# Second layer's sq and kv projections as seven quadrant products, with sums of the normalized input taken from PSUM

## The chip, the cores and the metric

The kernel runs on one core of a Trainium2 chip. The metric is the device time of one execution in microseconds (us); the lower, the better. TensorE (PE) multiplies matrices into PSUM, VectorE (DVE) and ScalarE (ACT) do elementwise work and read PSUM, GpSimd (POOL) does small arithmetic on SBUF and issues some DMAs, and SyncE (SP) issues all the others. Each engine works through its own list of instructions in order; semaphores make one wait for another.

## What is computed

Two layers of a decoder trunk with 512 tokens and width 1024, in float32. Each layer normalizes its input, projects it once to 3488 columns, hands these columns to four groups of heads, gates each group, and projects the result back onto the residual.

```python
def hybrid_layer(x, ...):
    h = rmsnorm(x, norm_g)
    p = h @ w_in                      # (512, 1024) @ (1024, 3488)
    (cq, ckv, kr, g_a, c_h, c_b, c_c, g_b, sg_u, sg_v, g_c, mq, mk, mv, g_d) = jnp.split(p, offs, axis=-1)
    ...                               # o_a latent attention, o_b convolution, o_c spatial gate, o_d block attention
    y = jnp.concatenate([o_a * silu(g_a), o_b * silu(g_b), o_c * silu(g_c), o_d * silu(g_d)], axis=-1)
    return y @ w_out                  # added to x
```

Every matrix operand is kept as a high and a low part (`split2`), and a product is three matmuls (`mm3`): high x high, high x low, low x high.

## The kernel before

**The order of the work.** The kernel is a list of chains (Python generators). While it is built, `Order` keeps a clock for each engine and lets the chain that is due go on, so the order of instructions on each engine is fixed before the run by this plan. `Chain.act`, `Chain.dve` and `Chain.pool` emit at line 162, `Chain.pe` at line 188; nearly every row of the profile has one of these lines, so rows are told apart by tile names. `Slots` hands out buffers.

**One layer.** `pre_norm` scales the tokens (tile `h`), transposes them on PE into PSUM (`hT`, from the two banks of `trS`) and splits them into `hTh` and `hTl`. `main` then issues the long projections. `cq` (416 columns) comes first, for each of the four tiles of 128 tokens; `low_chain`, `q_chain` and `kv_chain` follow behind it on the other engines, with short PE work of their own (`cT`, `q`, `kv` of a latent rank). After it `main` goes through `SEQ`: the token projections `sq` (columns of `sv` and `mq`) and `kv` (`mk` and `mv`), and 16 features of 128 columns each (`ga0`, `su0`, `ch0` and so on). A token projection is 4 tiles x 8 blocks of the inner dimension x 3 matmuls of 512 columns; a feature is 8 x 3 = 24 matmuls of 512 columns. Their sums stand in the three banks of `accS`.

**Beside it.** When all of cq's followers are done, `mla_heads` starts the latent attention (`t0a`, `t1a` transposes, `sa` scores, `pTa` transposed weights, `oa` output), and when mq, mk, mv and the latent heads are done, `moba_heads` starts the block attention (`tmqd`, `sd`, `pTd`, `od`). `mix_chain` prepares the spatial gate (`sgw`, `wsh`, `wsl`, `mp`). Their PE work is put between the projections' matmuls. `put_y` splits each gated output into `yTh`/`yTl` (tiles 0 to 5) or `yD` (6 and 7), and sends it to DRAM (`ysc`, line 858).

**The output product** (`seven`) is made of seven quadrant products already, in both layers: `b11`, `t3`, `b21`, `t4`, `t2`, `t1`, `b22`, in the banks `oz`, `ox`, `oy`. The sums of its weights (`t_sums`) are made in DRAM: SP copies a quadrant (line 324), POOL adds another with an accumulating DMA (line 330). The sums of its left side are made by `s_chain` from the y that it reads back from `ysc` (tiles `ys`, `sumh`, `suml`); they take the place of `hTh` and `hTl`, so they can't start before the last projection is issued.

**Weights.** `load_units` loads units of 512 KB in the order of use, on SP, into `raw` buffers (two of `rawS`, some in `tkS`). `split_units` makes `whi` and `wlo` of each, in halves, as soon as ACT and DVE have time by the plan or the unit is among the next four wanted; six pairs of buffers (`wS`) hold them. Three units of sq (`EARLY`) go to `yTh`/`yTl`, which are empty then.

Of the kernel before, what the change touches and what calls it, by code (L numbers as in the profile page):

```python
# [42 lines left out]
ZPROD = ("b11", "t3", "b21", "t4", "t2", "t1", "b22")  # L43
TS0 = 36000.0
TAIL = ((0, 256), (256, 512))

# [154 lines left out]
def hybrid_trunk(ctx: ExitStack, tc: tile.TileContext, x, positions, norm_g, w_c, w_f, w_t, w_o, mla_q_norm_g,  # L201
# [115 lines left out]

    def t_sums(l):

        for steps in ((("t1", "b11", "b12"), ("t3", "b12", "b22")), (("t2", "t1", "b22"),), (("t4", "t2", "b21"),)):  # L320
# [12 lines left out]
            yield o.now + 8000.0  # L333
# [6 lines left out]
    for l in range(DEPTH):  # L340
# [3 lines left out]
        add_unit(mla_w_ukv[l], 1, 512, f"ukv_{l}")  # L344
        for n in SEQ:
            if n in TOKS:
# [13 lines left out]
    def load_units():  # L360
        for u in order:
            ch = Chain(o)
            u.raw_slots = rawS
            if u.name in ("c2_0", "c3_0") or u.name[:-3] in ZPROD and u.name[-3] == "1":
# [191 lines left out]
    for l in range(DEPTH):  # L556
# [16 lines left out]
        L.seven = l in SEVEN  # L573
        L.hT_free, L.p1, L.h_done, L.h = Event(), Event(), [Event(), Event()], {}
        L.s = {n: [Event() for _ in range(4)] for n in ("t2", "t1", "b22")}
        L.left, L.s4 = {}, [Event(), Event()]
        L.QK_taken = False
        L.torder = (2, 3, 0, 1) if l and layers[l - 1].seven else (0, 1, 2, 3)
        L.x = [None] * NT
        for n in ("ga0", "ga1", "gd0", "gd1"):  # L580
            L.gate_ev[n] = Event()
        for j in range(2):
            L.u_ev[j] = Event()
            L.b_ev[j] = [Event() for _ in range(3)]
        layers.append(L)

# [8 lines left out]
    def pre_norm(L, t, xx, t0, release):  # L595
# [18 lines left out]
        def half(c):  # L614
# [12 lines left out]
            o.set(L.hT[t][c], c2.t)  # L627
        for c in range(2):
            o.spawn(half(c))

    def hk(L, k):
# [144 lines left out]
    def sv_chain(L, t, a, t0, put):  # L776
        ch = Chain(o, t0)
        l = L.l
        if t == 0:
            L.vn = [(yield from v4S.get(ch, f"vnh{l}", [P, NT, GW], F32R)),  # L780
# [19 lines left out]
    def mix_chain(L):  # L800
        ch = Chain(o)
        l = L.l
        sgw = yield from obS.get(ch, f"sgw{l}")
        sgw = sgw.rearrange("p (g s) -> p g s", g=4)
# [11 lines left out]
        for g2 in range(2):  # L816
            mp = yield from accS.get(ch, f"mp{g2}_{l}")
            for g in (2 * g2, 2 * g2 + 1):
# [7 lines left out]
            accS.put(c2)  # L826
        t2S.put(ch)
# [16 lines left out]
    def put_y(ch, L, kt, yv):  # L844
# [135 lines left out]
    def mqk_chain(nm):  # L980
        def f(L, t, a, t0, put):
            ch = Chain(o, t0)
            l = L.l
            gn = L.dq if nm == "mq" else L.dk
            if t == 0:
                L.MD[nm] = yield from ydS.get(ch, f"{nm}{l}", [P, NT, 4, 64], F32)
# [22 lines left out]
    def mv_chain(L, t, a, t0, put):  # L1009
        ch = Chain(o, t0)  # L1010
        if t % 2 == 0:
            L.Mt[t // 2] = yield from v4S.get(ch, f"Mt{t}_{L.l}", [P, 2, 4, P], F32R)
# [307 lines left out]
    def main():  # L1320
# [17 lines left out]
        def done_unit(name):  # L1338
            if units[name].slots is not eS:
                units[name].slots.put(m)  # L1340

        def seven(L):
            l = L.l
# [68 lines left out]
        for L in layers:  # L1412
# [19 lines left out]
            for n in SEQ:  # L1432
                if n in TOKS:
                    us = []
# [27 lines left out]
            for half in range(0 if L.seven else 2):  # L1462
# [17 lines left out]
                for group, cut in (((0, 1, 2), YCUT), ((3,), 0)) if half == 0 else (((t,), 0) for t in range(NT)):  # L1480
# [83 lines left out]
    if 0 in SEVEN:  # L1564
        o.spawn(t_sums(0), TS0, 4)
    o.spawn(start())
    o.run()
# [50 lines left out]
```

## Time and profile before

| | us |
|---|---|
| median of 3 runs (lowest, highest) | 498.12 (497.85, 498.44) |
| the profiled execution | 499.12 |
| its span, first to last instruction | 497.4 |
| second layer: cq starts on PE | 255.61 |
| sq starts | 282.66 |
| kv starts | 319.81 |
| first of su0 | 358.19 |
| last matmul of attention | 429.75 |
| output product starts | 455.71 |
| its fifth product (t2) starts | 477.47 |

The starts are from the chain of waits and the timeline of PE. The page gives each engine's busy time; the chain of waits goes back from the last instruction to what released each; windows give the busy time of each engine in a stretch, with the clock that PE was granted and the busy share of the 16 DMA engines. A row of the timeline has the start, the length, the engine, the line, the operation, the tile written and those read, the shape, how many in a row, and in brackets the idle time before it with what ended it. A row's length on PE is that of one matmul in the pipeline; the step from one start to the next is what counts for the sum.

### The profile page before, as it was taken

The page shows a single profiled execution, that of the slowest core. Times are in us where ns is not written, and L with a number is a line of the kernel's source. Part 1 is how long each engine was busy: PE and PEld are TensorE (multiplying, and loading weights), DVE is VectorE, ACT ScalarE, POOL GpSimd, SP SyncE. Part 2 cuts the span into 40 slices and gives each one's busy share as a digit, 9 for nine tenths or more (in the row PEclk, how much of TensorE's full clock was granted, in tenths as well). Part 3 has the DMA queues.
Part 4 walks back from the last instruction along what each step waited for, and adds up shares of the span by engine and source line. Part 5 has one row for each costly group of instructions (what it writes and reads, how often), then busy time and mean ns, then how long its engine had stood idle before and what let it go on. Part 6 is the DMA issues. An engine that isn't in the chain of part 4 may idle for free.

```text
span 497.4 us, 7832 instructions
## 1 busy us (share of the span) xinstructions
PE 486.4 (98%) x2448; PEld 412.5 (83%) x2448; DVE 386.0 (78%) x1008; ACT 317.0 (64%) x933; POOL 156.2 (31%) x328
## 2 busy tenths in 40 slices
PE   6899999999999999999999999999999999999997
PEld 4798878788888888888889988888888888888886
DVE  4877884777988788669898698677969788765992
ACT  5688753576777775446657896567758587524640
POOL 6867883656110000000031388463351000000000
PEclk9999999999999999999999999999999999999999
DMA  8545559444575235786474232664548528565642
GB/s 273 150 141 199 196 117 203 171 86 88 192 145 188 71 98 175 210 299 219 157 256 157 86 106 108 211 149 97 118 122 245 142 102 215 174 249 188 227 171 92
DMA packets 35339, 81.98 MB, mean 165 GB/s; under 512 B 7137, under 2 KB 16609, under 8 KB 35042
## 3 DMA queue, kind: packets, MB, share of 16 engines
q1 hardware_dynamic: 26818, 73.10, 42.7%
q0 software_dynamic: 8480, 8.39, 11.5%
q8 instruction: 19, 0.31, 0.3%
q14 instruction: 22, 0.18, 0.1%
HBM read 73.61 MB, written 24.64 MB: 198 GB/s over the span
## 4 chain that ended last, share of the span: by engine, by line
PE 87%; POOL 4%; ACT 3%; DMA 3%; DVE 2%; issue 1%; POOLq 0%; DVEq 0%
PE kv L188 7%; PE cq L188 6%; PE oy L188 6%; PE sq L188 5%; PE cb L188 4%; PE gd L188 4%; PE ch L188 4%; PE cc L188 4%; PE su L188 4%; PE gc L188 4%; PE gb L188 4%; PE ox L188 4%; PE oz L188 4%; PE sa L188 3%; PE ga L188 2%; PE od L188 2%
## 5 line engine op out<-in xcount | busy, mean ns | idle before, releaser
L162 ACT ACTIVATE pd<-pd,mnd 128x256 f32<-128x256 f32 (+3 forms) x50 | 26.9, 547 | 2.8 <-DVE mnd L162 2.3
L330 POOL DMA_DIRECT2D t<-in_w_o_dram x16 | 17.9, 1121 | 33.1 <-DMA t<-t 22.6
L162 ACT ACTIVATE pha<-pTa 128x512 fp32r<-128x512 f32 (+3 forms) x32 | 13.9, 436 | 20.0 <-PE pTa L188 19.8
L188 PE MATMUL kv<-whi_kv,hTh 128*128 128x512 f32 x64 | 26.1, 408 | 0.0
L188 PE MATMUL kv<-whi_kv,hTl 128*128 128x512 f32 x64 | 25.1, 392 | 0.0
L188 PE MATMUL kv<-wlo_kv,hTh 128*128 128x512 f32 x64 | 25.0, 391 | 0.0
L188 PE MATMUL cq<-whi_c,hTh 128*128 128x416 f32 x64 | 24.0, 376 | 0.0
L162 ACT ACTIVATE phd<-pTd 128x512 fp32r<-128x512 f32 (+3 forms) x32 | 13.8, 434 | 14.9 <-PE pTd L188 14.7
L162 ACT ACTIVATE pa<-pa,mna 128x256 f32<-128x256 f32 (+3 forms) x40 | 21.4, 542 | 2.5 <-DVE mna L162 2.4
L188 PE MATMUL cq<-whi_c,hTl 128*128 128x416 f32 x64 | 22.6, 353 | 0.0
L188 PE MATMUL cq<-wlo_c,hTh 128*128 128x416 f32 x64 | 22.5, 351 | 0.0
L162 DVE TENSOR_TENSOR wlo_t<-raw_t,whi_t 128x512 fp32r<-128x512 f32 x32 | 21.1, 691 | 0.0
L162 ACT ACTIVATE whi_t<-raw_t 128x512 fp32r<-128x512 f32 x32 | 18.2, 618 | 4.1 <-DMA raw_t<-t 4.1
L162 POOL TENSOR_SCALAR xss<-xss 128x1 f32<-128x1 f32 x8 | 3.8, 476 | 52.3 <-ACT jk L162 45.1
L162 DVE TENSOR_TENSOR pla<-pTa,pha 128x512 fp32r<-128x512 f32 (+3 forms) x32 | 15.2, 484 | 5.5 <-ACT pha L162 5.5
L188 PE MATMUL sq<-yTh,hTh 128*128 128x512 f32 x48 | 18.9, 393 | 0.0
L188 PE MATMUL sq<-yTh,hTl 128*128 128x512 f32 x48 | 18.7, 390 | 0.0
L162 DVE TENSOR_TENSOR pld<-pTd,phd 128x512 fp32r<-128x512 f32 (+3 forms) x32 | 15.2, 484 | 4.5 <-ACT phd L162 4.4
L188 PE MATMUL sq<-yTl,hTh 128*128 128x512 f32 x48 | 18.7, 390 | 0.0
L162 DVE CUSTOM_DVE_ANT_0 pa<-sa,maskb 128x512 f32<-128x512 f32 (+3 forms) x32 | 14.8, 484 | 5.0 <-PE pTa L188 4.2
L162 DVE TENSOR_TENSOR wlo_b<-raw_b,whi_b 128x512 fp32r<-128x512 f32 x24 | 16.0, 688 | 0.7 <-ACT whi_b L162 0.7
L162 DVE CUSTOM_DVE_ANT_0 pd<-sd,maskb 128x256 f32<-128x256 f32 (+3 forms) x32 | 15.0, 483 | 2.0 <-PE pTd L188 1.9
(377 smaller groups left out, 1853.0 us busy)
## 6 DMA issues: line engine op xcount, KB each, us to landing
t<-in_w_o_dram POOLq DMA_DIRECT2D x16, 512.0 KB, 6.2
raw_t<-t SPq DMA_DIRECT2D x16, 512.0 KB, 4.0
raw_b<-in_w_o_dram SPq DMA_DIRECT2D x12, 512.0 KB, 4.2
raw_sq<-in_w_t_dram SPq DMA_DIRECT2D x8, 512.0 KB, 3.5
t<-in_w_o_dram SPq DMA_DIRECT2D x8, 512.0 KB, 4.4
raw_kv<-in_w_t_dram SPq DMA_DIRECT2D x8, 512.0 KB, 3.6
t<-t SPq DMA_DIRECT2D x8, 512.0 KB, 4.8
ys<-ysc SPq DMA_DIRECT2D x14, 256.0 KB, 5.2
```

Source lines behind the costliest of these rows:

```text
L162: f(*a, **k)
L188: f(*a, **k)
L330: nc.gpsimd.dma_start(z_src(l, n, j), quad(l, b, j), accum_op=ALU.add, max_dma_last_dim=1024)
```

## The change

The first layer stays. In the second (`STOK = (1,)`) sq and kv together are one product of a 512 x 1024 left side h and a 1024 x 1024 right side W, cut into quadrants: h11 (tokens 0 to 255, inner 0 to 511), h12, h21 and h22, and of W b11, b21 (columns of sq) and b12, b22 (of kv). Seven products replace eight: p11 = h11 b11; p21 = h12 b21; p3 = (h11 - h21)(b12 + b22); p4 = h22 (b11 + b12 + b21 + b22); p2 = (h11 - h21 + h22)(b11 + b12 + b22), p1 = (h21 - h22)(b11 + b12), p22 = (h12 - h11 + h21 - h22) b22. Each is 2 tiles x 4 blocks x 3 matmuls of 512 columns.

Four features stand between the products: ga0, ga1, gd0 and ch0; the 12 others follow p22. The sums of W are made in DRAM by `t_sums`, under the first layer (from 110 us by the plan). The sums of h are made by DVE from the transposes in PSUM before their bank is given back (`h_sums`), and split later (`sum_split`) into `yTh`/`yTl`; so the early units of sq and a y of tiles 0 to 5 wait for that space. `p_out` combines products: for each of two tiles of 128 tokens it copies p11, p3 and p4 on ACT and takes two differences for p2 and one for p1 on DVE. The second half of each pair of weight units is loaded into the buffers of h (`hS`). The latent heads wait until p4 is issued, the spatial gate's start until p2 is, and its products use `trS`.

```diff
+STOK = (1,)
+SPROD = ("p11", "p21", "p3", "p4", "p2", "p1", "p22")
+SSUMS = {"p3": 0, "p2": 1, "p1": 2, "p22": 0}
+TSI = 110000.0
+SEQ1 = ["p11", "p21", "ga0", "p3", "ga1", "p4", "gd0", "p2", "ch0", "p1", "p22", "cc0", "gd1", "su0", "gc0",
+        "cb0", "gb0", "ch1", "cc1", "cb1", "gb1", "su1", "gc1"]
...
+            if u.name[:-3] in SPROD and u.name[-3] == "1":
+                u.raw_slots = hS
+                u.raw = yield from hS.get(ch, f"raw_{u.name}")
...
             yield from split2(c2, *(z[:, :, t * P:(t + 1) * P] for z in L.h[c]), tp.rearrange("p (k n) -> p k n", k=4))
+            o.set(L.hT[t][c], c2.t)
+            if L.stok:
+                yield from h_sums(c2, L, t % 2, (t // 2, c), tp)
             trS.put(c2)
...
+    def h_sums(ch, L, i, quadrant, tp):
+        f = L.f32
+        if quadrant == (1, 0):
+            f["a21", i] = yield from (yaS, zzS)[i].get(ch, f"a21_{i}")
+            f["a21", i] = f["a21", i][:, 0:512]
+            yield from ch.act(A.activation, f["a21", i], tp, AF.Copy)
...
+        if quadrant == (1, 1):
+            f["s1", i] = yield from t2S.get(ch, f"s1_{i}")
+            yield from ch.dve(V.tensor_tensor, f["s1", i], f["a21", i], tp, op=ALU.subtract)
...
+        elif quadrant == (0, 0):
+            w = f["w", i] = yield from t2S.get(ch, f"w_{i}")
+            yield from ch.dve(V.tensor_tensor, f["a21", i], tp, f["a21", i], op=ALU.subtract)
+            o.spawn(sum_split(L, "p3", i, f["a21", i], ch.t, (yaS, zzS)[i]), None, 5)
+            yield from ch.dve(V.tensor_tensor, w, tp, f["s1", i], op=ALU.subtract)
...
+        else:
+            s4 = yield from t2S.get(ch, f"s4_{i}")
+            yield from ch.dve(V.tensor_tensor, s4, tp, f["w", i], op=ALU.subtract)
+            o.spawn(sum_split(L, "p22", i, s4, ch.t, t2S.put), None, 5)
...
+    def sum_split(L, n, i, src, t0, put):
+        while n not in L.want and max(o.clk["A"], o.clk["V"]) > o.now + WSLACK:
+            yield o.now + 100.0
+        yield from split2(ch, *(z[:, :, i * P:(i + 1) * P] for z in p_sum(L, n)), src.rearrange("p (k n) -> p k n", k=4))
...
     def mix_chain(L):
+        if L.stok:
+            yield from ch.wait(L.mix_go)
...
     def put_y(ch, L, kt, yv):
+        if L.stok and kt < 6:
+            yield from ch.wait(L.st_done)
...
     def mla_heads(L):
+        if L.stok:
+            yield from ch0.wait(L.mla_go)
...
+        def p_out(L, n, i, a, st, t0, ev):
+            if n == "p11":
+                yield from ch.act(A.activation, f["p1", i], a, AF.Copy)
+            elif n == "p3":
+                yield from ch.act(A.activation, f["x", i], a, AF.Copy)
+            elif n == "p4":
+                yield from ch.act(A.activation, f["c", i], a, AF.Copy)
+            elif n == "p21":
+                users(L, "sq", i, a, ch.t, accS)
+            elif n == "p2":
+                yield from ch.dve(V.tensor_tensor, a, a, f["p1", i], op=ALU.subtract)
+                yield from ch.dve(V.tensor_tensor, c, c, a, op=ALU.subtract)
+                users(L, "sq", 2 + i, c, ch.t, t2S)
+            elif n == "p1":
+                yield from ch.dve(V.tensor_tensor, c, a, c, op=ALU.subtract)
+                users(L, "kv", 2 + i, c, ch.t, (yaS, zzS)[i])
+            else:
+                users(L, "kv", i, a, ch.t, accS)
...
-            early_put(m)
+            if l + 1 == DEPTH or l + 1 not in STOK:
+                early_put(m)
...
+    for l in STOK:
+        o.spawn(t_sums(l, p_src, p_src, "p", "p"), TSI, 4)
```

More of the change, by code (lines that the diff above doesn't have):

```diff
@@ L344, in hybrid_trunk @@
         add_unit(mla_w_ukv[l], 1, 512, f"ukv_{l}")
-        for n in SEQ:
-            if n in TOKS:
+        for n in SEQ1 if l in STOK else SEQ:
+            if n in SPROD:
+                for j in range(2):
+                    add_unit(p_src(l, n, j), 2, 512, f"{n}{j}_{l}")
+            elif n in TOKS:
                 for kq in range(4):
@@ L574, in hybrid_trunk @@
         L.hT_free, L.p1, L.h_done, L.h = Event(), Event(), [Event(), Event()], {}
+        L.stok, L.st_done, L.out_done, L.f32, L.mix_go, L.mla_go = l in STOK, Event(), Event(), {}, Event(), Event()
+        L.want = set()
+        L.ps = {n: [Event() for _ in range(2)] for n in SSUMS}
+        L.p3_done = Event()
         L.s = {n: [Event() for _ in range(4)] for n in ("t2", "t1", "b22")}
@@ L577, in hybrid_trunk @@
         L.QK_taken = False
-        L.torder = (2, 3, 0, 1) if l and layers[l - 1].seven else (0, 1, 2, 3)
+        L.torder = (2, 3, 0, 1) if l in STOK or l and layers[l - 1].seven else (0, 1, 2, 3)
         L.x = [None] * NT
@@ L584, in hybrid_trunk @@
             L.b_ev[j] = [Event() for _ in range(3)]
+        for i in range(2):
+            for e in ("ev", "ev1", "evw"):
+                L.f32[e, i] = Event()
+            L.f32["s1put", i] = shared(t2S, 2)
         layers.append(L)
@@ new lines, in sum_split @@
+    def sum_split(L, n, i, src, t0, put):
+        ch = Chain(o, t0)
+        if n == "p22":
+            yield from ch.wait(L.p3_done)
+        elif n != "p1":
+            yield from ch.wait(layers[L.l - 1].out_done)
+        while n not in L.want and max(o.clk["A"], o.clk["V"]) > o.now + WSLACK:
+            yield o.now + 100.0
+        ch.t = max(ch.t, o.now)
+        yield from split2(ch, *(z[:, :, i * P:(i + 1) * P] for z in p_sum(L, n)), src.rearrange("p (k n) -> p k n", k=4))
+        o.set(L.ps[n][i], ch.t)
+        if n == "p1":
+            put = L.f32["s1put", i]
+        (put.put if isinstance(put, Slots) else put)(ch)
@@ L778, in sv_chain @@
         l = L.l
-        if t == 0:
+        if "vn" not in L.f32:
+            L.f32["vn"] = True
             L.vn = [(yield from v4S.get(ch, f"vnh{l}", [P, NT, GW], F32R)),
@@ L1010, in mv_chain @@
         ch = Chain(o, t0)
-        if t % 2 == 0:
+        if t // 2 not in L.Mt:
+            L.Mt[t // 2] = None
             L.Mt[t // 2] = yield from v4S.get(ch, f"Mt{t}_{L.l}", [P, 2, 4, P], F32R)
@@ L1342, in seven, with users @@
+        def users(L, n, t, a, t0, slots):
+            put = shared(slots, 2)
+            for i, nm in enumerate(TOKS[n]):
+                o.spawn(fns[nm](L, t, a[:, i * 256:(i + 1) * 256], t0, put))
         def seven(L):
@@ L1431, in main @@
                             f"cb{j}": cb_chain(j), f"gb{j}": gb_chain(j)})
-            for n in SEQ:
-                if n in TOKS:
+            st = {"bank": {}, "ev": {}, "f32": {}}
+            for n in SEQ1 if L.stok else SEQ:
+                if n in SPROD:
+                    yield from product(L, n, st)
+                    if n == "p11":
+                        o.spawn(t_sums(l), None, 4)
+                    if n == "p22":
+                        o.spawn(load_residual(L), None, 3)
+                elif n in TOKS:
                     us = []
```

88 lines of the change are left out of this document (81 added, 7 removed).

## The prediction

> **What bounds the kernel now.** I read the page's busy shares first, then the chain of waits, then the windows, and took durations from the timeline last.
>
> ```profile
> PE 486.4 (98%) x2448; PEld 412.5 (83%) x2448; DVE 386.0 (78%) x1008; ACT 317.0 (64%) x933; POOL 156.2 (31%) x328
> ...
> PE 87%; POOL 4%; ACT 3%; DMA 3%; DVE 2%; issue 1%; POOLq 0%; DVEq 0%
> ```
>
> TensorE (PE) carries the chain. Its 98% is a share of modelled ends, so it can't say alone whether PE runs without gaps. The chain of waits, in order of time, says it (start, length, then how many matmuls):
>
> ```profile
> 288.89 17.70 PE sq L188 x78
> 306.60 8.84 PE ga L188 x39
> ...
> 438.92 5.44 PE gb L188 x24
> 444.36 5.44 PE su L188 x24
> ...
> 455.71 5.44 PE oz L188 x24
> ...
> 477.47 13.60 PE oy L188 x60
> ```
>
> Each start is the start above it plus its length. 78 matmuls of 512 columns in 17.70 us are 227 ns each, and 24 in 5.44 us are again 227 ns, in a stretch with attention beside it and in one without. So PE issues one such matmul each 227 ns and waits for nobody in the second layer's projections and output product. What a matmul less is worth there is its issue step of 227 ns, not the 390 ns that one lasts.
>
> The Trainium skill (Perfetto Trace Analysis, Identifying the Most-Contended Engine) calls matmul occupancy a bad measure and says to judge by the busy share of LDWEIGHTS. By that 83% PE would have 17% to spare and 24 matmuls less would be worth 5.44 x 0.83 = 4.5 us; the trace disagrees, since the window 440 to 450 below has 8.29 of 10 in weight loads although the chain shows no gap there, so 83% is a full stream of this shape.
>
> ```profile
> 250.00:355.00 105.00, 105.00 (x556) 91.94 (x555) 85.90 (x256) 74.80 (x275) 53.74 (x100) 1.00 0.49 141
> 440.00:450.00 10.00, 10.00 (x46) 8.29 (x45) 5.75 (x10) 2.55 (x5) 0.00 (x0) 1.00 0.44 150
> ```
>
> (Windows: length, then busy us of PE, weight loads, VectorE (DVE), ScalarE (ACT), GpSimd (POOL), the granted clock, the DMA share, GB/s.) From 250 to 355, where the change acts, DVE works 85.90 of 105 us and ACT 74.80. DVE is the engine next to bound.
>
> **What it takes away.** sq and kv are 2 x 4 tiles x 8 x 3 = 192 matmuls of 512 columns in the second layer; seven products are 7 x 2 x 4 x 3 = 168. Transposes, features, attention and the first layer's matmuls stay. 24 x 227 ns = 5.44 us, the very length of the row of su.
>
> **What it adds to DVE and ACT.** Prices are steps between neighbours in a queue with no idle time:
>
> ```profile
> 439.56 2.49 DVE L162 TENSOR_TENSOR wlo_b<-raw_b,whi_b 128x512 fp32r<-128x512 f32 x4
> ...
> 472.53 1.66 ACT L162 ACTIVATE whi_t<-raw_t 128x512 fp32r<-128x512 f32 x3
> ...
> 255.58 0.69 DVE L162 TENSOR_TENSOR hTl<-hT,hTh 128x512 fp32r<-128x512 f32 x1
> 256.18 0.58 DVE L162 TENSOR_TENSOR wlo_c<-raw_c,whi_c 128x416 fp32r<-128x416 f32 x1
> ```
>
> Four in 2.49 us with 0.69 for the last: 0.60 us a step on DVE; three in 1.66: 0.52 on ACT. A subtraction that reads PSUM (hTl) steps by 0.60 too. DVE gets 8 sums of h, 8 low halves of the sums, 12 low halves of six more weight units (14 for 8) and 6 combinations of products: 34 x 0.60 = 20.4 us. ACT gets 2 copies of a quadrant, 8 high halves, 12 of weights and 6 copies of products: 28 x 0.52 = 14.6 us. ACT has 30 us free from 250 to 355, so its part is put at nothing; should it come late, hTh and the copies of the first product are what PE would see. POOL gets 8 accumulating DMAs; its arithmetic is the same.
>
> Where does DVE's part show? Four places, each with both ends.
>
> (a) The sums stand between the splits of hT, and a transpose must wait for one of two PSUM banks that the sums now hold longer.
>
> ```profile
> 255.70:282.60 26.90, 26.90 (x155) 25.66 (x154) 22.44 (x54) 20.02 (x75) 6.78 (x10) 1.00 0.42 143
> ```
>
> Eight subtractions are 4.8 us, one split (wsl, 0.6) moves out, and DVE has 4.46 us idle in this stretch, most of it at the end. PE's order there is new: the transposes of the last tiles come after more cq matmuls. Between 0 (idle time takes it) and 4.2 (all of it on the path). Adding the queue up item by item I find two transposes 0.1 and 0.3 us late: 0.4.
>
> (b) From the second product on, weights are used twice as fast: a product takes 5.44 us and two units, where sq took 21.8 us for four. DVE's first work on a finished tile (the norm statistics of sv) waits for the second product; behind it in the queue stand the splits of p3 and ga1.
>
> ```profile
> 290.50 0.41 DVE L162 BATCH_NORM_STATS2 bst<-sq 128x6 f32<-128x256 f32 x1
> ...
> 303.60 0.34 DVE L162 SCALAR_TENSOR_TENSOR K<-K,mk,gk_b 128x64 f32<-128x64 f32 x1 [0.40 <-POOL mk L162]
> ...
> 307.26 0.34 DVE L162 SCALAR_TENSOR_TENSOR mq<-mq,mmq,dq_b 128x64 f32<-128x64 f32 x1 [0.71 <-POOL mmq L162]
> ```
>
> From those statistics to the last split of ga1 I count 15.4 us of DVE work in the new order, against 15.6 us of PE work from the end of that tile to the matmul that reads the split. Nothing to spare, and each wait for POOL (0.40, 0.71 above) would show. Upper end from the window 250 to 355: 85.90 + 20.4 = 106.3 us of DVE work against 105 - 5.44 = 99.6 of PE, 6.7 us too much, unless work moves behind. It does: attention can't start before p4 is issued and starts after p2; adding PE's steps in the new order that is 7 us later than now, and a head less is done when p22 ends. A head's DVE work is about 7 us: the two rows below, over eight heads, are 1.9 us each; scaling, the operands' splits and the sum of the output are the rest.
>
> ```profile
> L162 DVE TENSOR_TENSOR pla<-pTa,pha 128x512 fp32r<-128x512 f32 (+3 forms) x32 | 15.2, 484 | 5.5 <-ACT pha L162 5.5
> ...
> L162 DVE CUSTOM_DVE_ANT_0 pa<-sa,maskb 128x512 f32<-128x512 f32 (+3 forms) x32 | 14.8, 484 | 5.0 <-PE pTa L188 4.2
> ```
>
> (A row holds the four latent heads of both layers, so eight.) 0 to 6.7; I take 0.6, near the item count.
>
> (c) Attention now ends just ahead of the output product; before, 26 us of features followed it.
>
> ```profile
> 427.60 0.27 PE L188 MATMUL pTd<-ident,pd 128*128 128x128 f32 x1
> 427.91 0.28 ACT L162 ACTIVATE phd<-pTd 128x128 fp32r<-128x128 f32 x1 [0.20 <-PE pTd L188]
> 428.22 0.29 DVE L162 TENSOR_TENSOR pld<-pTd,phd 128x128 fp32r<-128x128 f32 x1 [0.81 <-ACT phd L162]
> ...
> 429.75 0.27 PE L188 MATMUL od<-pld,Mt 128*128 128x128 f32 x1
> 430.12 0.60 ACT L162 ACTIVATE obd<-od 64x512 f32<-64x512 f32 x1 [1.41 <-PE od L188]
> ...
> 432.85 0.69 DVE L162 TENSOR_TENSOR yD<-yad,yD 128x512 fp32r<-128x512 f32 x1 [0.70 <-ACT yD L162]
> ```
>
> From the last transpose to a usable pld are 0.9 us; the new order has three gc matmuls and two short od ones between (0.9 us). 0 to 1.2 (one 512-wide item ahead on ACT and on DVE); 0.3.
>
> (d) The last y then goes to DRAM and back for the sums of the output product. T is the start of that product.
>
> ```profile
> 474.94 0.69 DVE L162 TENSOR_TENSOR suml<-ys,sumh 128x512 fp32r<-128x512 f32 x1
> ...
> ysc<-yad SPq DMA_DIRECT2D x4, 256.0 KB, 4.7
> ...
> ys<-ysc SPq DMA_DIRECT2D x14, 256.0 KB, 5.2
> ...
> DMA to landing us min/median/max: 2.0/5.1/7.6
> ...
> DMA to landing us min/median/max: 3.6/5.2/5.9
> ```
>
> (The timeline, the DMA issues, and the landings of the tiles ysc and ys.) Now the last sum is done at 475.6, 1.8 us ahead of oy. After, DVE has 30 items of 0.60 and 14 of 0.34 us from T + 0.95 to the sum that oy needs at T + 23.6: done at T + 23.8. The store can be issued at about T + 5.3, when SP has passed the load of a t4 unit that waits for its buffer; with 4.7 and 5.2 us the read lands at T + 15.2, and DVE arrives at T + 14.2. So the sum is 0.2 us late if the read is early (2.0 and 3.6), 1.2 by the medians, 4.8 with the longest landings (7.6 and 5.9, T + 18.8). I take 0.9. Behind the waiting item stand the splits of t4 and t2, and PE waits for these.
>
> **DMA.** Eight more copies and eight accumulations in DRAM run under the first layer, about 110 to 215, and 6 units more load in the second.
>
> ```profile
> q1 hardware_dynamic: 26818, 73.10, 42.7%
> q0 software_dynamic: 8480, 8.39, 11.5%
> ...
> 110.00:215.00 105.00, 105.00 (x556) 88.99 (x555) 85.23 (x223) 69.85 (x167) 14.42 (x39) 1.00 0.52 148
> 80.00:90.00 10.00, 10.00 (x46) 8.28 (x45) 3.60 (x9) 4.19 (x15) 2.62 (x6) 1.00 0.89 227
> ```
>
> Sixteen accumulations took 11.5% of 497.4 = 57 us, 3.6 each; the other queue 2.9 us per MB, 1.5 a unit. 8 x (3.6 + 1.5) = 41 us on top of 0.52 x 105 = 55: 96 of 105 us. At 0.89 busy, with the same kind of transfers, PE loses nothing (window 80 to 90), and loads run units ahead: 0. Without that cover a load that lands 2 us late costs 2 us. SP stands in line behind copies that wait for accumulations; POOL has 14 us of work in those 105, so its waiting for copies holds up little.
>
> **Sum.** -5.44 + 0.4 + 0.6 + 0.3 + 0.9 = -3.2 us. The profiled execution took 499.12 us (span 497.4 and 1.7 around it), 1.0 above the runs' median of 498.12; it would take 495.9. On the median: 494.9 us.
>
> **Rivals.** *Full gain*: idle time takes all, 498.12 - 5.44 = 492.7. For it: PE had no gap anywhere in the second layer though DVE was full near 255 to 267; against: (b) and (d) have no margin in my count. *Gain eaten at the end*: (d) at its upper 4.8, the rest as forecast: 498.12 - 5.44 + 1.3 + 4.8 = 498.8, no change. For it: one in-order queue waits for a round trip through DRAM; against: both landings would have to be the longest. *VectorE becomes the bound (slower)*: its place is from the sums to p22; if attention's work doesn't fall behind, 6.7 us there, and with (a), (c) and (d): 498.12 - 5.44 + 6.7 + 1.6 = 501.0. It decides from about 5 us on. For it: 106.3 against 99.6; against: the later start of attention. The Trainium skill (TensorE: Matmul & The Clock Gate, Part 1) says that after an idle window of about 3.4 us the array runs at half rate for about as long; by that a single wait of such a length would cost an estimated 1.7 us more, 502.7, and no run here shows it (the clock column is 1.00 in each window). *It doesn't do what it says*: the built order has 24 matmuls fewer, so no.
>
> **How the numbers follow.** Forecast (waits of 1 to 4.4 us in all, 493.7 to 497.1) 56%, full gain (under 1 us) 26%, eaten 9%, slower 9%. From no change I can tell 0.2%, 1.0 us: faster below 497.1. Faster 0.82, same 0.09, slower 0.09. The range is from 492.5, just under the full gain, to 497.8; the likeliest case's own is 493.7 to 497.1.
>
> **What would show it.** Right: 24 fewer matmuls, rows of x24 still 5.44, cq to oz shorter by 5 us less a fraction, DVE busy about 406 and ACT 331 us. (a): idle time of hT's weight load put down to DVE s or w. (b): px or ga waiting for wlo_p3, wlo_ga. (c): od waiting for pld. (d): a DVE wait of ys for DMA at T + 14, and oy for suml. The forecast is wrong if PE waits over 4.4 us, if a wait shows in the first layer, or if the clock falls below 1.00.

## The result, and the profile after

| | before | after |
|---|---|---|
| median of 4 runs (lowest, highest), us | 498.25 (497.85, 498.44) | 504.16 (502.85, 505.03) |
| ratio to before, 95% interval | | 1.0117 (1.0093 to 1.0142) |
| span of the profiled execution | 497.4 | 501.1 |

The change made the kernel 1.2% slower; the forecast was 0.6% faster. The two profiled executions lie closer together than the medians, since the one of before (499.12) is some 0.9 above its median and the one of after (502.85) is the fastest of its four.

The page of the kernel after, its busy shares and the shares of the chain of waits:

```profile
PE 484.5 (97%) x2424; PEld 407.1 (81%) x2424; DVE 405.8 (81%) x1037; ACT 330.1 (66%) x960; POOL 174.3 (35%) x342
...
PE 61%; DVE 16%; DMA 8%; ACT 7%; POOL 4%; issue 3%; SPq 1%; DVEq 0%; POOLq 0%; ACTq 0%
```

The 24 matmuls are gone, and the totals of DVE (405.8) and ACT (330.1) came out as forecast (406 and 331). POOL's rose from 156.2 to 174.3. The only addition to it that the forecast named, the issue of eight accumulating DMAs, is 9.1 of these 18.1 us by the page (row of `p<-in_w_t_dram`, x8); the rest is looked at below. And PE's share of the chain fell from 87% to 61%: the end is no longer set by PE alone.

Where the time went is read from four starts on PE, in both kernels (timeline of PE; first before, then after):

```profile
216.24 0.39 PE L188 MATMUL oz<-whi_b,yTh 128*128 128x512 f32 x1
255.61 0.43 PE L188 MATMUL cq<-whi_c,hTh 128*128 128x416 f32 x1
455.55 0.39 PE L188 MATMUL oz<-whi_b,yTh 128*128 128x512 f32 x1
```

```profile
214.99 0.39 PE L194 MATMUL oz<-whi_b,yTh 128*128 128x512 f32 x1
257.20 0.35 PE L194 MATMUL cq<-whi_c,hTh 128*128 128x416 f32 x1
282.54 0.40 PE L194 MATMUL pz<-whi_p,hTh 128*128 128x512 f32 x1
457.47 0.45 PE L194 MATMUL oz<-whi_b,yTh 128*128 128x512 f32 x1
```

| stretch on PE, us | before | after | difference |
|---|---|---|---|
| start to the first layer's output product (oz) | 216.2 | 215.0 | -1.2 |
| oz to the second layer's cq | 39.4 | 42.2 | +2.8 |
| cq to the second output product | 199.9 | 200.3 | +0.3, where -5.4 was due: 5.8 of waits |
| output product to the end | 41.8 | 43.7 | +1.8 |
| span | 497.4 | 501.1 | +3.7 |

The -1.2 is no gain of the change: it is one wait of the first layer in the profiled execution of before (list of PE's waits: total, times, longest), which the same instructions don't show in other executions (214.9 in before_sums_80 below).

```profile
PE t0a L188 <- DVE Q L162: 1.1, 1, 1.1
```

From cq to the second output product PE has 589 matmuls of 512 columns after and 613 before, 24 less, so the saving of 5.4 was there. Against it stood 2.8 + 5.8 + 1.8 = 10.4 us of lost time, where 2.2 were forecast. The same list of after:

```profile
PE t0a L194 <- POOL Q L168: 1.8, 1, 1.8
PE oy L194 <- DVE xr L168: 1.8, 2, 1.0
...
PE hT L194 <- ACT a L168: 1.2, 1, 1.2
PE ox L194 <- DVE wlo_t L168: 1.0, 1, 1.0
...
PE oz L194 <- DVE wlo_b L168: 0.5, 1, 0.5
PE pz L194 <- ACT pz L168: 0.5, 1, 0.5
...
PE sa L194 <- DVE lo1a L168: 0.2, 1, 0.2
```

oz, ox and one of the two oy are in the first layer. There the chain of waits of after runs through two reads of y:

```profile
212.44 0.69 DVE wlo_t L168
214.09 5.82 DMA ys<-ysc
219.93 11.91 DMA ys<-ysc
```

The queue of SP and the one of POOL (timeline of each, after) show what these reads met:

```profile
208.41 0.47 SPq L338 DMA_DIRECT2D p<-p  x1
213.15 0.33 SPq L271 DMA_DIRECT2D raw_t<-t  x1
213.57 0.47 SPq L338 DMA_DIRECT2D p<-p  x1
214.09 3.93 SPq L271 DMA_DIRECT2D ys<-ysc  x6
```

```profile
214.83 1.08 POOL L344 DMA_DIRECT2D p<-in_w_t_dram  x1 [11.91 <-DMA p<-p]
219.61 1.03 POOL L344 DMA_DIRECT2D p<-in_w_t_dram  x1 [3.70 <-DMA p<-p]
```

The last two copies for the sums of W stood in SP's queue among the output product's loads, and the two accumulations that wait for them ran with the reads of y. From 200 to 250 us the reads landed after 5.8 / 7.9 / 11.9 us (shortest, median, longest; 3.7 / 5.2 / 5.7 before), DVE stood idle 4.2 us for them, and the splits queued behind its waiting item (wlo_b, wlo_t) came late to PE. SP issued the reads no later than before (214.1 to 219.9; before, 214.8 to 220.1), so what grew is the time from issue to landing. The busy share of the DMA engines was 1.16 and 1.10 in the two windows of 5 us from 220 (before: 0.98 and 0.23). Whether the copy or the accumulation holds up the reads was not separated.

### The profile page after: what moved, and what is told of

The parts are those of the page before. It is cut to its first block, busy times and chain, and to the rows that moved or that the text cites. A ratio compares the mean times of both kernels' runs of the same rounds, so it can differ in the third digit from the quotient of the medians.

```text
span 501.1 us, 7879 instructions
## 1 busy us (share of the span) xinstructions
PE 484.5 (97%) x2424; PEld 407.1 (81%) x2424; DVE 405.8 (81%) x1037; ACT 330.1 (66%) x960; POOL 174.3 (35%) x342
## 4 chain that ended last, share of the span: by engine, by line
PE 61%; DVE 16%; DMA 8%; ACT 7%; POOL 4%; issue 3%; SPq 1%; DVEq 0%; POOLq 0%; ACTq 0%
PE kv L194 5%; DMA ys<-ysc 5%; PE cc L194 4%; PE cb L194 4%; PE gb L194 4%; PE su L194 4%; PE cq L194 4%; ACT junk L168 4%; PE gd L194 3%; PE ch L194 3%; PE gc L194 3%; PE oy L194 3%; PE sa L194 3%; DVE wlo_t L168 2%; PE sd L194 2%
## 5 line engine op out<-in xcount | busy, mean ns | idle before, releaser
L168 ACT ACTIVATE pha<-pTa 128x512 fp32r<-128x512 f32 (+3 forms) x32 | 13.9, 435 | 18.1 <-PE pTa L194 17.7
L168 ACT ACTIVATE pa<-pa,mna 128x256 f32<-128x256 f32 (+3 forms) x43 | 22.7, 540 | 1.6 <-DVE mna L168 1.4
L344 POOL DMA_DIRECT2D p<-in_w_t_dram x8 | 9.1, 1389 | 41.8 <-DMA p<-p 41.8
L168 ACT ACTIVATE whi_t<-raw_t 128x512 fp32r<-128x512 f32 x31 | 18.1, 619 | 4.6 <-DMA raw_t<-t 4.4
L168 DVE TENSOR_TENSOR wlo_p<-raw_p,whi_p 128x512 fp32r<-128x512 f32 x28 | 19.6, 709 | 0.5 <-ACT whi_p L168 0.4
L168 ACT ACTIVATE whi_p<-raw_p 128x512 fp32r<-128x512 f32 x25 | 15.0, 625 | 2.3 <-DMA raw_p<-p 2.3
L168 POOL TENSOR_SCALAR rope_scratch<-rope_scratch 128x64 f32<-128x64 f32 x30 | 13.9, 479 | 2.3
L194 PE MATMUL oy<-whi_t,sumh 128*128 128x512 f32 x32 | 12.7, 395 | 1.8 <-DVE xr L168 1.8
L168 ACT ACTIVATE whi_b<-raw_b 128x512 fp32r<-128x512 f32 x22 | 13.2, 623 | 1.6 <-DMA raw_b<-in_w_o_dram 1.6
```

The source lines that it names most:

```text
L168: f(*a, **k)
L194: f(*a, **k)
```

## The experiments

The starts on PE of all kernels, by the same four stretches (pz is sq in a kernel with the old products). From sums_80 on in this table, every kernel begins the sums of W at 80 us, and its edit is made to sums_80. The saving of 5.4 would put cq to oz at 194.5.

| | to oz | oz to cq | cq to oz | of it from pz | oz to end | median, us | ratio (95%) |
|---|---|---|---|---|---|---|---|
| before | 216.2 | 39.4 | 199.9 | 173.1 | 41.8 | 498.25 | 1 |
| after | 215.0 | 42.2 | 200.3 | 174.9 | 43.7 | 504.16 | 1.0117 (1.0093 to 1.0142) |
| again | 214.3 | 42.4 | 200.7 | 175.4 | 43.7 | 503.01 | 1.0109 (1.0094 to 1.0124) |
| no_sums | 214.6 | 39.0 | 202.5 | 177.2 | 43.8 | 499.69 | 1.0049 (1.0028 to 1.0070) |
| before_sums | 215.5 | 44.2 | 199.9 | 173.0 | 41.9 | 502.83 | 1.0096 (1.0077 to 1.0114) |
| before_sums_80 | 214.9 | 39.4 | 199.9 | 173.0 | 42.0 | 498.10 | 0.9999 (0.9990 to 1.0009) |
| sums_80 | 215.1 | 39.0 | 200.4 | 175.1 | 44.1 | 501.09 | 1.0073 (1.0052 to 1.0095) |
| copy_first | 215.7 | 39.0 | 209.1 | 186.5 | 49.6 | 517.07 | 1.0378 (1.0351 to 1.0406) |
| plain_h | 215.8 | 39.4 | 196.0 | 169.2 | 43.8 | 496.58 | 0.9966 (0.9955 to 0.9977) |
| no_wlo | 214.6 | 39.0 | 197.3 | 172.0 | 44.3 | 497.60 | 0.9986 (0.9976 to 0.9995) |
| late_output_sums | 214.9 | 39.5 | 204.9 | 179.6 | 44.3 | 504.98 | 1.0142 (1.0121 to 1.0164) |
| ys_pool | 216.6 | 39.0 | 200.5 | 175.1 | 45.4 | 501.14 | 1.0071 (1.0048 to 1.0094) |
| late_mix | 215.5 | 39.0 | 200.8 | 175.5 | 42.5 | 499.52 | 1.0024 (1.0013 to 1.0036) |
| late_mix_2 | 214.8 | 39.0 | 200.4 | 175.1 | 42.5 | 498.82 | 1.0016 (1.0004 to 1.0027) |
| spread | 215.1 | 39.0 | 197.0 | 171.6 | 43.2 | 496.95 | 0.9978 (0.9967 to 0.9990) |
| copy_dve | 215.8 | 39.0 | 199.0 | 173.7 | 43.5 | 498.31 | 1.0003 (0.9994 to 1.0012) |

The stretches are of one profiled execution each; the medians are over all executions of a kernel. rope_dve is left out of the table, since part of its work is missing (below).

### The same kernel again

> The changed kernel unchanged. In its profiled execution the stretch from the start of the first layer's output product (oz) to the second layer's cq took 42.2 us (39.4 in the kernel before), cq to the second output product 200.3 (200.0, where 5.4 less was forecast), the rest 43.6 (41.8). If these waits are in the order of the instructions, they come again: 503 to 505 us, stretches within 0.5 us of those. If they were an accident of one execution, the stretches come out elsewhere or near 39.4 and 195.

503.01 us, with the stretches at 42.4, 200.7 and 43.7: the waits are in the order of the instructions.

### The first layer: without the sums of W, and with nothing but them

no_sums:

```diff
...
-        return psum_w[l, n][j] if len(n) == 2 else w_t[l, int(n[2]) - 1, 2 * int(n[1]) - 2 + j]
+        n = {"p1": "b11", "p2": "b11", "p3": "b12", "p4": "b22"}.get(n, f"b{n[1:]}")
+        return w_t[l, int(n[2]) - 1, 2 * int(n[1]) - 2 + j]
...
-    for l in STOK:
-        o.spawn(t_sums(l, p_src, p_src, "p", "p"), TSI, 4)
```

> The four sums of weights for the second layer's products are not made: p1 and p2 load quadrant b11, p3 b12 and p4 b22 in their place (so sq and kv come out as other numbers). Everything else is as in the changed kernel, 16 DMAs less. Theory 1, the sums' last copies and accumulations collide with the first layer's reads of y: the stretch from oz to cq falls from 42.2 to 39.4 us, the longest landing of a ys from 11.9 to about 6 us, and the time by 2.8 us to about 501.3. Rival, the tail is late because the units of the early weights are gone and DVE has more to do there: the stretch stays at 42, the time within 0.5 us of 504.2.

before_sums, on the kernel before, with `t_sums` taking its sources as in the change:

```diff
         o.spawn(t_sums(0), TS0, 4)
+    for l in (1,):
+        o.spawn(t_sums(l, p_src, p_src, "p", "p"), 110000.0, 4)
```

> The kernel before, with the eight copies and eight accumulations for the second layer's sums added from 110 us of the plan; nothing reads them, the output is as before. Theory 1: the transfers alone cost the first layer's tail 2 to 3 us, 500.5 to 501. Rival: the first layer is not touched by transfers, 498.2 (within 0.5).

no_sums is back at 39.0, its reads of y land after 5.5 us at the longest, and it is 3.3 us under the same kernel with sums (again). before_sums, with no product changed, lost 5.0 us (497.84 beside it), all of it between oz and cq (44.2). That is more than either theory gave it. The timeline of PE in before_sums shows why:

```profile
227.51 0.61 PE L188 MATMUL oz<-whi_b,yD 128*128 128x512 f32 x2
230.20 0.70 PE L188 MATMUL oz<-wlo_b,yD 128*128 128x512 f32 x1 [2.08 <-DVE wlo_b L162]
230.70 0.63 PE L188 MATMUL oz<-whi_b,yD 128*128 128x512 f32 x1
231.12 0.63 PE L188 MATMUL oz<-whi_b,yTh 128*128 128x512 f32 x1
...
233.26 0.62 PE L188 MATMUL oz<-whi_b,yTl 128*128 128x512 f32 x1
233.69 0.43 PE L188 MATMUL oz<-whi_b,yD 128*128 128x512 f32 x1
```

Behind a wait of 2.08 us the matmuls of 512 columns start every 430 ns, not every 227, until 233.69; the window of these five microseconds has the granted clock, 0.66, in its third column from the end:

```profile
230.00:235.00 5.00, 4.80 (x14) 3.81 (x15) 4.80 (x11) 3.13 (x6) 0.00 (x0) 0.66 0.82 234
```

Eight matmuls take 3.49 us (230.20 to 233.69) where 8 x 0.227 = 1.8 are due, another 1.7 us. The low half came late because DVE itself had stood idle for a read of y until 228.78 (timeline of DVE). So in this execution the late read was paid for twice.

### The same sums, earlier

sums_80 (after) and before_sums_80 (before_sums):

```diff
-TSI = 110000.0
+TSI = 80000.0
```

> The changed kernel with the sums of weights begun at 80 us of the plan in place of 110 (the last copies are then issued ahead of the load of gc1, not between t4 and ys). Theory 1: the stretch from oz to cq goes back to 39.4 to 40 us, the time to 501 to 501.7. Rival, any eight sums under the first layer cost this much wherever they stand: no gain, within 0.5 us of the changed kernel run beside it.

> before_sums with the sums begun at 80 us of the plan, ahead of the output product's loads. Theory 1 (place, not amount): the 5.0 us that before_sums lost come back, 498.2 to 499. Rival (amount): 501 or more.

The last accumulation is now issued ahead of the output product (timeline of POOL, sums_80, then before_sums_80):

```profile
187.23 1.10 POOL L344 DMA_DIRECT2D p<-in_w_t_dram  x1 [10.21 <-DMA p<-p]
```

```profile
186.72 1.03 POOL L338 DMA_DIRECT2D p<-in_w_t_dram  x1 [9.73 <-DMA p<-p]
```

Both have the old stretch (39.0 and 39.4). In the kernel before, the sixteen DMAs then cost nothing (0.9999). So it was their place, not their amount. In the changed kernel the move is worth 1.9 us (503.01 in again, 501.09). sums_80 is still 0.7% slower than before, and this is the second layer's part.

### The copy ahead of the split

Timeline of ACT after, around the third pair of transposes:

```profile
261.67 0.60 ACT L168 ACTIVATE hTh<-hT 128x512 fp32r<-128x512 f32 x1 [0.49 <-PE hT L194]
262.16 0.59 ACT L168 ACTIVATE a<-hT 128x512 f32<-128x512 f32 x1
```

The copy a, of an older transpose, stands behind the high half of the newest one, and the next transposes need its bank.

```diff
+            if L.stok and (t // 2, c) == (1, 0):
+                yield from h_sums(c2, L, t % 2, (t // 2, c), tp)
...
             o.set(L.hT[t][c], c2.t)
-            if L.stok:
+            if L.stok and (t // 2, c) != (1, 0):
```

> sums_80 with the copy of a transpose (a, ACT) ahead of that transpose's split, not behind it. Theory 2, the third transposes wait 1.18 us for this copy because it stands on ACT behind the high half of the transposes that PE issues just before: that wait goes, the second layer's stretch from cq to the output product is shorter by 1 to 1.5 us (200.4 to 199), the time 500 or so. Rival, VectorE (s, hTl) holds the bank and ACT is only what came last: the wait stays and is put down to DVE, no gain.

517.07 us. The wait moved to DVE (hT for hTl, 0.7), as the rival said, and the plan that follows from the move is another one far down:

```profile
PE px L194 <- DVE vn L168: 4.1, 2, 3.2
PE pTa L194 <- ACT mix L168: 2.5, 2, 1.6
...
```

This kernel's output is wrong, in a part that was not traced, so only the first wait is read from it. Whether ACT or DVE holds the bank longer stays open; in plain_h below, without either, the wait is gone.

### POOL or DVE ahead of the latent heads

late_output_sums:

```diff
-                    if n == "p11":
+                    if n == "p4":
                         o.spawn(t_sums(l), None, 4)
```

> sums_80 with the sums of the second layer's output weights begun after p4 in place of p11, so four accumulating DMAs of 1.0 us each on POOL no longer stand between the rotations of Q. Theory 3, POOL is what the latent heads wait for (t0a for Q: 1.2 to 1.8 us, the clock gate behind it in some executions): the wait goes, 1.2 to 1.5 us off the stretch from cq to the output product. Rival, DVE is late for the heads too (sa for lo1a, 0.7): the wait moves there, less than 0.5 us gained.

rope_dve:

```diff
-        on_dve = o.clk["V"] + ROPEB < max(o.clk["G"], ch.t)
+        on_dve = o.clk["V"] + ROPEB < max(o.clk["G"], ch.t) or name[0] == "q" and name[-1] == "1"
```

> sums_80 with the rotation of Q in the second layer on DVE alone (24 short instructions, some 0.15 us each, off POOL). Theory 3: t0a no longer waits for POOL. Theory 4, DVE is the engine that is short between the products, as in the rival of the prediction: 3.6 us more on DVE come back as waits of px, ga or sa for a low half, and the stretch from cq to the output product is no shorter or longer than 200.4.

In late_output_sums t0a waits for nobody, and yet the kernel is 3.9 us slower than sums_80. The heads start 1.8 us earlier (t0a at 327.6, 329.4 in sums_80) and wait inside (waits of PE), with the granted clock down to 0.58 behind them (window):

```profile
PE oa L194 <- DVE pla L168: 1.1, 1, 1.1
PE pTa L194 <- ACT mix L168: 0.9, 1, 0.9
PE pTa L194 <- DVE lo1a L168: 0.7, 1, 0.7
```

```profile
370.00:375.00 5.00, 5.00 (x17) 4.08 (x16) 3.88 (x9) 2.00 (x5) 3.02 (x8) 0.58 0.20 26
```

So the four DMAs did have a part in t0a's wait, but taking them away gained nothing: the waits moved further in, as the rival said, at a higher price than it gave. rope_dve tells little: with this order 134 matmuls, 126 of them of the output product and 8 of the block attention, are not issued, so neither its 486.21 us nor its stretches compare with anything. What can be read is that t0a waits there for Q on DVE (1.0 us).

### Less work on DVE

plain_h leaves out the sums of h, no_wlo the low halves of the products' weights.

```diff
-            if L.stok:
-                yield from h_sums(c2, L, t % 2, (t // 2, c), tp)
...
-                if n in SSUMS:
-                    yield from m.wait(L.ps[n][i])
...
```

```diff
-                yield from c2.dve(V.tensor_tensor, lo, raw, hi.bitcast(F32), op=ALU.subtract)
+                if u.name[:-3] not in SPROD:
+                    yield from c2.dve(V.tensor_tensor, lo, raw, hi.bitcast(F32), op=ALU.subtract)
+            if u.name[:-3] in SPROD:
+                u.lo = u.hi
```

> sums_80 without the sums of h: p3, p2, p1 and p22 multiply plain quadrants of h (so sq and kv come out as other numbers); gone are 8 sums and 8 low halves on DVE (9.6 us) and 2 copies and 8 high halves on ACT. If the sums' hold on the banks is what the transposes wait for (step a): the wait of 1.18 us goes, the stretch from cq to pz falls from 25.4 to 24 us or less. If DVE's load is what the heads wait for (t0a 1.2, sa 0.7): these go too, and cq to oz falls by 3 us or more; if POOL's rotations are, t0a's wait stays.

> sums_80 without the low halves of the products' weights: the high half is multiplied in their place (other numbers come out), 28 DVE instructions of 0.60 us less, 16.8 us, all between cq and p22; PE's work is the same. Theory 4, DVE is short there: pz to oz falls by 2 us or more from 175.0, and the waits of t0a and sa go. Rival, theory 3, POOL alone: t0a still waits over 1 us for POOL's Q, and the stretch falls by less than 1 us.

Both took away the waits of t0a and sa, for POOL's Q too, although POOL has as many of Q's rotations to do in plain_h and two more of each step in no_wlo: 4.4 us (plain_h) and 3.1 us (no_wlo) off cq to oz, against sums_80. In plain_h the wait of hT for a is gone as well; its stretch from cq to pz is longer (26.9 us), since more of the latent projections stands ahead of pz there, so the whole from cq to oz is what can be compared. The windows from 311 to 336 us of before, after, no_wlo and plain_h, in this order (busy us of PE, weight loads, DVE, ACT, POOL in 25):

```profile
311.00:336.00 25.00, 25.00 (x138) 21.52 (x137) 17.25 (x50) 15.39 (x44) 12.83 (x28) 1.00 0.67 181
```

```profile
311.00:336.00 25.00, 23.24 (x108) 19.08 (x107) 24.36 (x52) 16.61 (x34) 24.09 (x39) 1.00 0.89 227
```

```profile
311.00:336.00 25.00, 25.00 (x119) 20.89 (x118) 19.28 (x49) 15.43 (x42) 15.66 (x33) 1.00 0.98 247
```

```profile
311.00:336.00 25.00, 25.00 (x125) 21.12 (x124) 18.05 (x44) 14.58 (x35) 10.93 (x24) 1.00 1.00 241
```

After, DVE is busy 24.36 and POOL 24.09 of 25 us. With DVE at 19.28 (no_wlo), POOL is at 15.66; a part of this is that the rotations of Q lie earlier there (to 323.8) and in plain_h (to 315.1) than after (316.9 to 333.5). How one drags the other is in the durations of POOL's rotations of Q in this part (shortest / median / longest, ns), before and after:

```profile
L162 POOL TENSOR_TENSOR Q<-Q,cosT x6: 316/328/613, 286.7 to 314.7; 128x64 f32<-128x64 f32 x6
L162 POOL TENSOR_TENSOR Q<-Q,rbq x6: 318/320/767, 288.4 to 315.7; 128x64 f32<-128x64 f32 x6
```

```profile
L168 POOL TENSOR_TENSOR Q<-Q,cosT x6: 318/740/1135, 318.7 to 332.3; 128x64 f32<-128x64 f32 x6
L168 POOL TENSOR_TENSOR Q<-Q,rbq x6: 318/771/1366, 319.4 to 333.5; 128x64 f32<-128x64 f32 x6
```

The same six instructions, with the same shortest time, take more than twice as long at the median beside a full DVE: about the 0.68 us of one of DVE's subtractions of 512 columns. Side by side (timeline, after), the two engines take turns:

```profile
322.69 1.41 DVE L168 TENSOR_TENSOR yTl<-w,yTh 128x512 fp32r<-128x512 f32 x2
324.02 2.94 DVE L168 TENSOR_TENSOR wlo_p<-raw_p,whi_p 128x512 fp32r<-128x512 f32 x4
```

```profile
322.73 1.56 POOL L168 TENSOR_TENSOR Q<-Q,cosT 128x64 f32<-128x64 f32 x2
324.24 1.50 POOL L168 TENSOR_TENSOR Q<-Q,rbq 128x64 f32<-128x64 f32 x2
```

Two of POOL's rotations take about as long as two of DVE's subtractions, and end 0.2 us behind them. Of the eighteen rotations of Q on POOL after, thirteen last over 0.6 us, and ten of these end 0.16 to 0.2 us behind the end of a DVE instruction. DVE pays too: four low halves take 2.94 us here, where the four that gave the forecast its price of 0.60 took 2.49, in a stretch in which POOL did nothing. The Trainium skill (SBUF — State Buffer, SBUF: two separate sides) says that DVE with two inputs in SBUF and GpSimd share a pair of ports as an exclusive lock, held for a whole instruction. The medians agree with it, and so do these rows. No run here tells this lock from another resource that the two could take in turns.

### The last stretch

ys_pool, in the second layer only:

```diff
-        yield from ch.dve(V.tensor_tensor, a[:, 256:512], b[:, 256:512], a[:, 256:512], op=ALU.add)
+        yield from ch.pool(G.tensor_tensor, a[:, 256:512], b[:, 256:512], a[:, 256:512], op=ALU.add)
```

(and the two sums behind it alike)

> sums_80 with the twelve sums of the read-back y in the second layer's output product on POOL (idle there) in place of DVE: 12 x 0.34 = 4.1 us off DVE. Theory 5, the output product ends late because DVE is full from its start (oy waits 1.0 us for xr, no wait of DVE for a transfer): that wait goes, 1.0 to 1.6 us off the last stretch (44.1 against 41.8 in the kernel before). Rival, the last y's round trip through DRAM sets it: the wait stays, put down to suml or a DMA.

The last stretch grew to 45.4. Neither theory had the reason: a sum of 256 columns that takes 0.42 us on DVE takes 1.18 on POOL, and oz now waits 1.2 us for wlo_b (tile ys, ys_pool):

```profile
L168 POOL TENSOR_TENSOR ys<-ys,ys x6: 742/1182/2008, 458.5 to 475.1; 128x256 f32<-128x256 f32 x6
```

late_mix moves features only:

```diff
-SEQ1 = ["p11", "p21", "ga0", "p3", "ga1", "p4", "gd0", "p2", "ch0", "p1", "p22", "cc0", "gd1", "su0", "gc0",
-        "cb0", "gb0", "ch1", "cc1", "cb1", "gb1", "su1", "gc1"]
+SEQ1 = ["p11", "p21", "ga0", "p3", "ga1", "p4", "gd0", "p2", "ch0", "p1", "p22", "gc1", "su1", "cb1", "gb0",
+        "cc0", "cb0", "gb1", "ch1", "su0", "cc1", "gc0", "gd1"]
```

> sums_80 with the twelve features behind p22 in another order: gc1, su1, cb1, gb0, cc0, cb0, gb1, ch1, su0, cc1, gc0, gd1 (before: cc0, gd1, su0, gc0, cb0, gb0, ch1, cc1, cb1, gb1, su1, gc1), so that gd1, which needs only the block heads' own output, is last and the mixer's gate is not. If the last stretch is long because the last feature's gate, split and store stand in DVE's queue ahead of the output product's sums: that stretch falls from 44.1 towards 42, the time by 1 to 2.5 us to some 499. If it is DVE's load from whatever comes before: no change, 501.

> late_mix once more, beside spread on the same chip: 499.5, ratio 1.002 to the kernel before; its stretch from pz to oz 175.4.

42.5 us instead of 44.1 in both runs, oy waits no more, and the times (499.52 and 498.82) are within 0.3% of before. So the order of the features behind p22, and with it what stood in DVE's queue at the start of the output product, set its end.

### Another order of the same work

spread:

```diff
-SEQ1 = ["p11", "p21", "ga0", "p3", "ga1", "p4", "gd0", "p2", "ch0", "p1", "p22", "cc0", "gd1", "su0", "gc0",
-        "cb0", "gb0", "ch1", "cc1", "cb1", "gb1", "su1", "gc1"]
+SEQ1 = ["p11", "p21", "gc0", "su0", "p3", "p4", "gd0", "p2", "ga0", "p1", "cc1", "p22", "ga1", "ch1",
+        "cc0", "cb1", "gb1", "ch0", "cb0", "su1", "gc1", "gb0", "gd1"]
-TSI = 110000.0
+TSI = 80000.0
...
-            if n == "p2":
+            if n == "p3":
                 o.set(L.mix_go, o.now)
-            if n == "p4":
+            if n == "p2":
                 o.set(L.mla_go, o.now)
...
-                    if n == "p11":
+                    if n == "p2":
                         o.spawn(t_sums(l), None, 4)
...
-        on_dve = o.clk["V"] + ROPEB < max(o.clk["G"], ch.t)
+        on_dve = o.clk["V"] + (ROPEB if name[-1] == "0" else 1500.0) < max(o.clk["G"], ch.t)
```

> sums_80 with two features between p21 and p3 (gc0, su0), one each before p2, p1 and p22 (gd0, ga0, cc1), the others behind, gd1 last; the latent heads wait for p2 (before: p4), the sums of the output's weights begin after p2 (before: after p11), and Q's rotations go to DVE only where it is 1.5 us ahead of POOL. Theory 4, DVE and POOL fall behind because seven products follow one another with a feature each: with more PE work ahead of p3 and the heads later, t0a's and sa's waits (1.2 and 0.7) go, pz to oz falls by 1.3 us or more from late_mix's 175.4, and the time to 498 or below. Rival, the waits only move to other instructions between p21 and oz: 499 to 500.

> As spread in kind (gd0, ga1 between p21 and p3, su0, ch1 and cb0 before p2, p1 and p22, gd1 last, heads after p3), and the copy of p11 made by DVE in place of ACT. The accumulation of p21 waited 0.46 us for that copy: this wait goes if ACT's queue was its cause; 0.6 us more DVE work per copy stands against it. 498 to 499.

496.95 us, 0.9978 (0.9967 to 0.9990) of before: by 0.2% it beats the kernel before too, with all sums, splits and products of the change in it. The waits of the second layer that are left (list of PE's waits), and its window of 311 to 336:

```profile
PE hT L193 <- ACT a L167: 1.2, 1, 1.2
...
PE pz L193 <- ACT pz L167: 0.5, 1, 0.5
```

```profile
311.00:336.00 25.00, 25.00 (x116) 20.70 (x115) 24.96 (x50) 16.76 (x42) 21.06 (x37) 1.00 0.59 200
```

DVE is as full as in after (24.96 of 25), and in this window PE waits for nobody: between p21 and p3 it has two features to issue that need none of the items in DVE's queue. But spread also moves the start of the heads, of the spatial gate and of the output's sums, and makes all of Q's rotations on POOL, whose medians are 370, 643 and 375 ns there (cosT, rbq and sinT; 740, 771 and 680 after). Which of these moves gave how much was not separated. copy_dve, of the same kind, came out at 498.31, no different from before; its wait for the copy of p11 went, and px waits 0.5 us each for wlo_p and whi_p.

## Why the prediction was wrong

The saving was right: 24 matmuls, 5.44 us (cq to oz is 3.9 us shorter than before in plain_h and 2.9 in spread, with some of the waits still there). The sum of the waits was wrong: 2.2 forecast, 10.4 in the profiled execution. Two steps failed: DMA, put at 0, and the waits from cq to the output product, put at 1.3 for (a), (b) and (c) together, where 5.8 were lost.

- **DMA, taken as 0, was 2.8 to 4.8 us.** By the medians it is 1.9 (again to sums_80) to 5.0 (before_sums). This step failed outright: a term put at nothing. The reason given was that at a busy share of 0.89 PE loses nothing and that loads run units ahead. This holds for weights. The read-back of y is no load that runs ahead: it can't start before y is stored, and its sums are wanted in the same output product. I costed the transfers in the stretch of the plan (110 to 215 us), and named that SP stands in line, but didn't follow the last copies through SP's queue: issued at 208 and 214, they put their accumulations at 214.8 and 219.6, on top of the reads. The rule of the prediction itself, "a load that lands 2 us late costs 2 us", would have pointed at the cost.
- **(a), taken as 0.4, was 1.2 by the list of waits.** The place and the range (0 to 4.2) were right; the holder by the profile is ACT's copy, whose cost I had put at nothing, not the subtractions on DVE.
- **(b), taken as 0.6, was 0.5 + 1.8 + 0.2 by the list.** The shortage was where I put it, between p21 and p22, but not at the splits of p3 and ga1. pz waited for the copy of p11 on ACT (named as the sign of a late ACT), and the latent heads for Q on POOL. no_wlo and plain_h, with less on DVE, took this last wait away. That POOL's "arithmetic is the same" counted instructions: six of each step of Q's rotations as before, but at a median of 740 in place of 328 ns (cosT), and DVE's subtractions were priced at 0.60 us from a stretch without POOL, where four beside POOL took 2.94. And the window from 250 to 355, 106.3 us of work against 99.6, doesn't show the 25 us in which DVE and POOL are both full.
- **(c), taken as 0.3:** no such wait in the list.
- **(d), taken as 0.9, was 1.0 by the list, 1.8 by the stretch.** The size fits; the mechanism was another. DVE never waited for a transfer there, it was simply full, and PE waited for xr to free a bank, not for suml.

These named waits of (a) and (b) are 3.7 of the 5.8 us in cq to oz. Each is followed by 0.2 to 0.3 us until the matmuls are back in step, some 0.9 together; the other 1.2 us are not accounted for.

Of the rivals, "VectorE becomes the bound" (501.0, 9%) was near in place and price for the second layer: sums_80, which has only that part, is at 501.09. That the number fits so well is luck in part: PE's longest waits there are put down to ACT's copy and POOL's Q (1.2 each), not to DVE's low halves. No rival held the first layer's tail. The estimate from the clock gate (+1.7) stood beside that rival; half rate behind a wait did come, in several executions.

## What to carry to other kernels

A transfer that an in-order queue issues late does its harm where it lands, not where the plan starts it: follow the last of a new group through the queue to its issue time, and ask which short round trip is under way there. An engine's busy share has to be read over the stretch of its worst 25 us, and with the engines that slow down beside it; the price of an instruction there is not the one from a quiet stretch, on either engine. A full engine need cost nothing as long as PE has work that needs none of its items: the same products and splits, in another order and with POOL taking more of the rotations, were worth 4 us here (sums_80 to spread).

## What the runs showed of the hardware

**Half rate after one wait of 2 us.** In before_sums one wait of 2.08 us was followed by eight matmuls at some 430 ns. A wait of 1.76 us in after (t0a) was not: the granted clock is 1.00 from 335 to 340. The Trainium skill (TensorE: Matmul & The Clock Gate, Part 1) gives an idle window of about 3.4 us for this; the measured wait was shorter. Which part of a window PE has to be idle was not tried.

**Executions of one kernel differ by up to 3 us.** The kernel before ranged over 1.5 us in 29 runs beside spread (497.40 to 498.90), after over 2.2 in four (502.85 to 505.03), no_sums over 3.0 in six (499.26 to 502.24), and spread, with few waits, over 2.9 in twelve (495.89 to 498.79). In no_sums a part may be the clock: its profiled execution (501.64) has a wait of 1.85 us for lo1a and a granted clock of 0.78 in the five microseconds around it. What sets the spread of the others is not shown.

**POOL's small instructions stretch beside DVE, and DVE's beside them.** A rotation of 64 columns went from 0.33 to 0.74 us at the median; a sum of 256 columns in ys_pool took 0.74 at the shortest and 1.18 at the median. Four of DVE's subtractions of 512 columns went from 2.49 to 2.94 us.
